# Seven products for eight in one half of the gate and up projections of a float32 decoder trunk

## Chip, core and metric

One NeuronCore of a Trainium2 chip runs the whole program in one launch. The metric is the device time of one execution in microseconds (us), weights and inputs read from HBM. The engines are called PE (TensorE), DVE (VectorE), ACT (ScalarE), POOL (GpSimd) and SP (SyncE, which issues nearly all DMAs) in the profile's rows.

## What is computed

256 tokens of width 1024 go through two layers. Each layer has a half-step SwiGLU feed-forward step, a mixing step with two kinds of attention, a second feed-forward step of the same form, and a gated input embedding. All is float32.

```python
def swiglu(x, w_gate, w_up, w_down):
    return (jax.nn.silu(x @ w_gate) * (x @ w_up)) @ w_down

def hybrid_layer(h, p_i, ...):          # D_MODEL = 1024, D_FF = 2816, DEPTH = 2
    h = h + 0.5 * swiglu(rms_norm(h, ffn1_norm), ffn1_w_gate, ffn1_w_up, ffn1_w_down)
    ...                                  # mixing: projections, two attentions, w_out
    h = h + 0.5 * swiglu(rms_norm(h, ffn2_norm), ffn2_w_gate, ffn2_w_up, ffn2_w_down)
    gate = jax.nn.sigmoid(rms_norm(h, ple_norm) @ w_ple_gate)
    h = h + gate * (p_i @ w_ple_proj)
    return h
```

## The kernel before

**Matmuls.** A float32 operand is split in two: a high part rounded to fp32r (`wh`, by ACT) and the rest (`wl`, by DVE). `mm3` (L213 to L220) issues three matmuls of 512 columns for one product: high by high (L217), low by high and high by low (L218, L219; `x` split alike into `h` and `l`). The tokens (128 at a time, one half `t` of the 256) are stationary, the weights are the moving operand.

**Weights.** All weights lie in HBM in units of 128 x 2048, in the order of use. `Unit.load` (L120) brings a piece of 128 x 1024 into one of 7 raw buffers (L128, queue of SP), and splits it into one of 8 pairs `wh`, `wl` (L132 on ACT, L133 on DVE). So ACT and DVE can be up to eight pieces ahead of PE, and the DMAs up to seven pieces ahead of them. A raw buffer is free again when DVE has split it; a pair is free again when PE has used it.

**A feed-forward step** (`ffn`, L482). The four steps are called a0, b0 (layer 0) and a1, b1 (layer 1). The 2816 columns of gate and up are worked in five blocks of 512 and a last one of 256. A block runs over K = 1024 in 8 chunks of 128 and over two halves of the tokens: 16 `mm3` into the banks `g` of PSUM and 16 into the banks `u`, 96 matmuls. `gated` (L485) applies silu on ACT and multiplies on DVE (`pr`, L491); `Gates.add` (L453) has PE transpose the result (four transposes `ft` for each half of tokens) and splits it into `fh`, `fl` for the down projection. `soon` puts such late work behind a number of matmuls.

**Sevens.** Three blocks (1 to 3) of the down projection already go as seven products for eight: with a 2 x 2 partition of weights and of gates, `Seven.operands` (L177) makes the weights' seven operands from four raw pieces with four sums on DVE (L168, in the raw buffers) and seven splits (L173, L174), `Gates.sums` (L409) makes the sums of the gates, and the products add up in seven banks of PSUM over the three blocks. Each product of a block is two `mm3`, six matmuls.

**Order.** Each engine and queue runs its own list in order. The lists are set when the program is built: a scheduler places the instructions engine by engine, so that a matmul of later work can stand ahead of one that would wait. PSUM has 8 banks, taken in turn.

## Time and profile before

| | |
|---|---|
| three runs | 1017.68, 1017.71, 1018.44 us (median 1017.71) |
| the profiled execution | 1019.1 us, of it 1017.3 us span from the first to the last instruction |
| TensorE's granted clock | 0.997 on the mean, 1.00 in the feed-forward steps |
| PE busy | 1004.5 us (99%) in 5106 matmuls and transposes |
| DVE busy | 753.1 us (74%) |
| ACT busy | 618.8 us (61%) |
| DMA | 187.41 MB, mean 184 GB/s |

The profile is of one execution; its times are us from the start of the span. An engine's row gives the start of an instruction and how long it took until its result was there. The engines take up the next instruction before that, so what an instruction costs an engine that never waits is the distance between the starts of two neighbours, and busy times of PE are no measure of what its matmuls cost.

### The profile page before, as it was taken

What the parts mean: (1) busy time and instruction counts of PE and PEld (TensorE: products, weight loads), DVE (VectorE), ACT (ScalarE), POOL (GpSimd) and SP (SyncE); (2) the same over time, 40 slices, a digit from 0 to 9 for tenths busy, and PEclk for the clock granted to TensorE, in tenths of its full rate; (3) what the DMA queues carried; (4) which work ended last, traced back from release to release, by engine and by line L of the source; (5) the groups of instructions that cost most, each with busy time, mean ns of one, the idle gap of its engine ahead of it and who ended that gap; (6) DMA issues with size and microseconds to landing.
All of it is one profiled execution on the core that took longest, in us unless ns stands there. A gap on an engine that the chain in (4) does not pass through costs nothing.

```text
span 1017.3 us, 13800 instructions
## 1 busy us (share of the span) xinstructions
PE 1004.5 (99%) x5106; PEld 849.9 (84%) x5106; DVE 753.1 (74%) x1051; ACT 618.8 (61%) x950; POOL 8.4 (1%) x13
## 2 busy tenths in 40 slices
PE   9999999999999999999999999999999999999996
PEld 7888888899888888888888888888998888888885
DVE  5776789976766666799865667899676756678994
ACT  5855566767575555557764555656766745556663
POOL 0000000000100000000000000000010000000000
PEclk9999999999999999999999999999999999999998
DMA  9875346674246555456765554557623465544641
GB/s 316 319 269 187 125 151 225 221 249 149 84 145 209 184 187 175 135 177 228 235 208 181 182 177 135 186 192 264 228 84 125 153 219 184 186 149 138 214 154 43
DMA packets 53492, 187.41 MB, mean 184 GB/s; under 512 B 6064, under 2 KB 6192, under 8 KB 53424
## 3 DMA queue, kind: packets, MB, share of 16 engines
q1 hardware_dynamic: 52992, 185.95, 54.2%
q8 instruction: 40, 0.66, 0.3%
q10 hardware_dynamic: 432, 0.57, 0.2%
q14 instruction: 28, 0.23, 0.1%
HBM read 185.45 MB, written 1.05 MB: 183 GB/s over the span
## 4 chain that ended last, share of the span: by engine, by line
PE 96%; DMA 2%; ACT 1%; DVE 0%; issue 0%; SPq 0%; ACTq 0%
PE g_a L217 4%; PE g_a L219 4%; PE g_b L219 4%; PE g_b L217 4%; PE g_b L218 4%; PE g_a L218 4%; PE u_a L217 4%; PE u_b L217 4%; PE u_a L218 4%; PE u_b L218 4%; PE u_b L219 4%; PE u_a L219 4%; PE d_b L219 3%; PE d_b L218 3%; PE d_b L217 3%; PE d_a L219 2%
## 5 line engine op out<-in xcount | busy, mean ns | idle before, releaser
L133 DVE TENSOR_TENSOR wl<-raw,wh 128x1024 fp32r<-128x1024 f32 (+1 forms) x306 | 362.3, 1197 | 161.0 <-ACT wh L132 159.5
L132 ACT ACTIVATE wh<-raw 128x1024 fp32r<-128x1024 f32 (+1 forms) x306 | 313.5, 1036 | 187.1 <-PE u_b L219 43.8
L173 ACT ACTIVATE wh<-raw 128x1024 fp32r<-128x1024 f32 x84 | 88.5, 1061 | 77.3 <-DVE raw L168 35.9
L174 DVE TENSOR_TENSOR wl<-raw,wh 128x1024 fp32r<-128x1024 f32 x84 | 100.4, 1221 | 11.7 <-ACT wh L173 11.0
L168 DVE TENSOR_TENSOR raw<-raw,raw 128x1024 f32<-128x1024 f32 x48 | 58.6, 1221 | 14.4 <-DMA raw<-in_w 12.1
L217 PE MATMUL d_a<-wh,fh_a 128*128 128x512 f32 x108 | 42.7, 396 | 0.0
L217 PE MATMUL d_b<-wh,fh_b 128*128 128x512 f32 x108 | 42.7, 396 | 0.0
L219 PE MATMUL d_b<-wh,fl_b 128*128 128x512 f32 x108 | 42.1, 390 | 0.0
L219 PE MATMUL d_a<-wh,fl_a 128*128 128x512 f32 x108 | 42.1, 390 | 0.0
L218 PE MATMUL d_a<-wl,fh_a 128*128 128x512 f32 x108 | 42.1, 389 | 0.0
L218 PE MATMUL d_b<-wl,fh_b 128*128 128x512 f32 x108 | 42.1, 389 | 0.0
L217 PE MATMUL g_a<-wh,x0h 128*128 128x512 f32 x96 | 38.0, 398 | 1.1 <-ACT x0h L262 1.1
L217 PE MATMUL g_b<-wh,x_mix0h 128*128 128x512 f32 x96 | 38.4, 400 | 0.0
L217 PE MATMUL g_b<-wh,x_mix1h 128*128 128x512 f32 x96 | 38.4, 400 | 0.0
L217 PE MATMUL g_a<-wh,xe0h 128*128 128x512 f32 x96 | 38.4, 400 | 0.0
L219 PE MATMUL g_a<-wh,xe0l 128*128 128x512 f32 x96 | 37.6, 391 | 0.0
L219 PE MATMUL g_b<-wh,x_mix1l 128*128 128x512 f32 x96 | 37.5, 390 | 0.0
L219 PE MATMUL g_b<-wh,x_mix0l 128*128 128x512 f32 x96 | 37.5, 390 | 0.0
L218 PE MATMUL g_b<-wl,x_mix0h 128*128 128x512 f32 x96 | 37.4, 390 | 0.0
L218 PE MATMUL g_b<-wl,x_mix1h 128*128 128x512 f32 x96 | 37.4, 390 | 0.0
L218 PE MATMUL g_a<-wl,xe0h 128*128 128x512 f32 x96 | 37.4, 390 | 0.0
L219 PE MATMUL g_a<-wh,x0l 128*128 128x512 f32 x96 | 37.3, 390 | 0.0
(454 smaller groups left out, 2551.2 us busy)
## 6 DMA issues: line engine op xcount, KB each, us to landing
raw<-in_w SPq DMA_DIRECT2D x338, 512.0 KB, 4.2
raw<-in_w SPq DMA_DIRECT2D x16, 256.0 KB, 5.2
xin<-in_xT SPq DMA_DIRECT2D x4, 256.0 KB, 5.3
h<-in_xr SPq DMA_DIRECT2D x2, 512.0 KB, 9.2
p<-in_pT SPq DMA_DIRECT2D x2, 256.0 KB, 4.9
fg<-in_fgain SPq DMA_DIRECT2D x1, 512.0 KB, 4.8
out_h<-hg SPq DMA_DIRECT2D x2, 256.0 KB, 2.3
out_h<-hg ACTq DMA_DIRECT2D x2, 256.0 KB, 2.7
```

What stands on the lines that cost most here:

```text
L132: nc.scalar.activation(wh[:, a], r[:, a], AF.Copy),
L133: nc.vector.tensor_tensor(wl[:, a], r[:, a], wh[:, a].bitcast(F32), ALU.subtract),
L168: nc.vector.tensor_tensor(self.raw[o], self.raw[a], self.raw[b], op)
L173: newest_wh[0] = nc.scalar.activation(wh, r, AF.Copy)
L174: nc.vector.tensor_tensor(wl, r, wh.bitcast(F32), ALU.subtract)
L217: nc.tensor.matmul(o, ah, bh, start=start, stop=False, **kw)
L218: nc.tensor.matmul(o, ah, bl, start=False, stop=False, **kw)
L219: newest_mm[0] = nc.tensor.matmul(o, al, bh, start=False, stop=stop, **kw)
```

## The change

In step a0 block 3, and in each of the other three steps blocks 1 and 3, the first half of K (chunks 0 to 3) is worked as seven products for eight. The partition is 2 x 2: the weights by K (256 and 256 rows) and by gate and up (512 and 512 columns), x by K and by token half. Seven products of two `mm3` take the place of eight.

`operands_own_first` loads the four pieces and yields the operands in the order 1, 7, 6, 5, 2, 4, 3. Products 1, 7, 6, 5 start banks of their own. Product 2 is added to bank `p1`, product 4 to `p7`, product 3 to `p5`, once the bank's first content has been read: ACT copies `p1` to `u`; DVE adds `p6` to it, makes `v` = `u` + `p7`, and `e` = `p5` - `v` (`u` and `v` are the halves of the tile printed as `ch`, `e` is in `cl`). The second half of K (chunks 4 to 7) goes on as before, 48 matmuls, and adds on to the same banks: gate on to `p1` and `p7`, up on to `p5` and a new bank `c22`. Three more sums on DVE then give the gate's second half and the two halves of up.

`x_sums` runs once in each step: one sum of the two parts of x over chunks 0 to 3, four sums of 128 x 256 on DVE, two splits on each of ACT and DVE. The weights' units are packed in the order of the new pieces; their number stays.

```diff
--- before.py
+++ after.py
@@ -30,6 +30,13 @@
 
 
 SEVEN = (1, 2, 3)
+
+
+def wide_sevens(first):
+
+    return (3,) if first else (1, 3)
+
+
 
 F_TAGS = ("sbq", "sbk", "v", "vm", "n0h", "n0l", "n1h", "n1l", "f4h", "f4l", "f5h", "f5l")
 
@@ -190,6 +197,25 @@
             self.sum(b21, b11, b21)
             yield 4, self.parts(b21)
 
+        def operands_own_first(self):
+
+            b11, b12, b21, b22 = range(4)
+            self.load(b11)
+            yield 1, self.parts(b11)
+            self.load(b12)
+            self.load(b22)
+            self.sum(b12, b12, b22)
+            yield 7, self.parts(b12)
+            self.sum(b11, b11, b12)
+            yield 6, self.parts(b11)
+            self.sum(b12, b11, b22, ALU.subtract)
+            yield 5, self.parts(b12)
+            self.load(b21)
+            yield 2, self.parts(b21)
+            self.sum(b11, b11, b21)
+            yield 4, self.parts(b11)
+            yield 3, self.parts(b22)
+
 
     due = []
     pe = [0.0]
@@ -493,8 +519,73 @@
 
             return silu, rest
 
+        xs = []
+
+        def x_sums():
+
+            v = f_p.tile([P, 4, T], F32, tag="f5h", name=f"xf_{tag}")
+            xh, xl = (q[:, 0:4].bitcast(F32) for q in x)
+            nc.vector.tensor_tensor(v, xh, xl, ALU.add)
+            a11, a12, a21, a22 = (v[:, k : k + 2, t * P : (t + 1) * P] for t in range(2) for k in (0, 2))
+            two = [wt(f"w{2 + k}", f"xsum{k}_{tag}") for k in range(2)]
+            s1, s2, s3, s4 = (two[k // 2][:, k % 2].rearrange("p (a b) -> p a b", a=2) for k in range(4))
+            nc.vector.tensor_tensor(s1, a21, a22, ALU.subtract)
+            nc.vector.tensor_tensor(s2, s1, a11, ALU.subtract)
+            nc.vector.tensor_tensor(s3, a11, a21, ALU.subtract)
+            nc.vector.tensor_tensor(s4, s2, a12, ALU.add)
+            xs.extend(f_p.tile([P, 4, T], F32R, tag=f"f4{q}", name=f"xs{q}_{tag}") for q in "hl")
+            for k in range(2):
+                sh, sl = (q[:, 2 * k : 2 * k + 2] for q in xs)
+                nc.scalar.activation(sh, two[k], AF.Copy)
+                nc.vector.tensor_tensor(sl, two[k], sh.bitcast(F32), ALU.subtract)
+
+        def x_of(p, j):
+            if p in (1, 2, 4):
+                return tok(x, j + 2 * (p != 1), int(p == 4))
+            return both(xs, slice(None), {5: 0, 6: 1, 7: 2, 3: 3}[p], slice(j * P, (j + 1) * P))
+
+        def wide_seven(i):
+
+            if not xs:
+                x_sums()
+            p = {k: bank(f"p{k}_{tag}{i}") for k in (1, 7, 6, 5)}
+            e2 = tuple(f_p.tile([P, 4, T], F32, tag=f"f5{q}", name=f"c{q}_{tag}{i}").rearrange("p a b -> p (a b)") for q in "hl")
+            u, v, e = e2[0][:, :512], e2[0][:, 512:], e2[1][:, :512]
+            own = (1, 7, 6, 5)
+            to = {**p, 2: p[1], 4: p[7], 3: p[5]}
+            for q, (wh, wl) in Seven().operands_own_first():
+                for j in range(2):
+                    c = slice(j * 512, (j + 1) * 512)
+                    mm3(to[q], x_of(q, j), (wh[:, c], wl[:, c]), q in own and j == 0, q in own and j == 1, skip_group_check=True)
+                if q == 1:
+                    nc.scalar.copy(u, p[1])
+                elif q == 6:
+                    nc.vector.tensor_tensor(u, u, p[6], ALU.add)
+                    nc.vector.tensor_tensor(v, u, p[7], ALU.add)
+                elif q == 5:
+                    nc.vector.tensor_tensor(e, p[5], v, ALU.subtract)
+            c22 = bank(f"c22_{tag}{i}")
+
+            def half_mm(u, banks):
+                for k in range(4):
+                    for t in range(2):
+                        mm3(banks[t], tok(x, 4 + k, t), u.at(k, 0, 512), banks[t] is c22 and k == 0, k == 3, skip_group_check=True)
+
+            ug, uu = Unit(4), Unit(4)
+            half_mm(ug, (p[1], p[7]))
+            nc.vector.tensor_tensor(v, u, p[7], ALU.add)
+            rests = [gated(i, 0, p[1], u)[1], gated(i, 1, v, e)[1]]
+            half_mm(uu, (p[5], c22))
+            nc.vector.tensor_tensor(u, p[5], u, ALU.subtract)
+            nc.vector.tensor_tensor(e, e, c22, ALU.add)
+            for r in rests:
+                r(1.4)
+
         for i in range(NBLK):
             last = i == NBLK - 1
+            if i in wide_sevens(feed is not None):
+                wide_seven(i)
+                continue
             g = [bank(f"g_{tag}_{i}{t}") for t in range(2)]
             sub = {"sub": 2} if feed and i == 0 else {}
             wg = wide([Unit(4, **sub) for _ in range(2)])
@@ -1005,6 +1096,10 @@
             wg, wu, wd = (i[f"{n}_w_{s}"][L] for s in ("gate", "up", "down"))
             for j in range(NBLK - 1):
                 m = ar(512 * j, 512 * j + 512)
+                if j in wide_sevens(L == 0 and n == "ffn1"):
+                    units.extend(np.concatenate([cols(v[k : k + 256], m) for v in (wg, wu)], axis=1) for k in (0, 256))
+                    units.extend(cols(v[512:], m) for v in (wg, wu))
+                    continue
                 wide(wg, m)
                 wide(wu, m)
             m = ar(DFF - 256, DFF)
```

Three places in the engines' lists, in the program before and in the changed one. The lines of the changed kernel are other numbers for the same code (L133 is now L140, L174 is L181, L168 is L175, L217 to L219 are L243 to L245, L491 is L517, L468 is L494, L262 is L288).

DVE in step b0, from the gating of block 0 (`pr`) on, before:

```order
L491 SCALAR_TENSOR_TENSOR pr_b0_00_3047<-u_b0_00_2871,hr_mix0_2754,s_b0_00_2971 128x512
L491 SCALAR_TENSOR_TENSOR pr_b0_01_3051<-u_b0_01_2872,hr_mix0_2754,s_b0_01_2973 128x512
L133 TENSOR_TENSOR wl54_1_0_129_3202<-raw54_1_0_129_3203,wh54_1_0_129_3201 128x1024
L468 TENSOR_TENSOR fl_b0_0_3050<-ft_b0_00_3069,fh_b0_0_3049 128x4x128
L133 TENSOR_TENSOR wl55_0_0_130_3230<-raw55_0_0_130_3231,wh55_0_0_130_3229 128x1024
L468 TENSOR_TENSOR fl_b0_0_3050<-ft_b0_01_3082,fh_b0_0_3049 128x4x128
L133 TENSOR_TENSOR wl55_1_0_131_3275<-raw55_1_0_131_3276,wh55_1_0_131_3274 128x1024
```

and now:

```order
L517 SCALAR_TENSOR_TENSOR pr_b0_00_3081<-u_b0_00_2905,hr_mix0_2788,s_b0_00_3005 128x512
L517 SCALAR_TENSOR_TENSOR pr_b0_01_3085<-u_b0_01_2906,hr_mix0_2788,s_b0_01_3007 128x512
L181 TENSOR_TENSOR wl7_51_0_130_3188<-raw7_51_0_3107,wh7_51_0_130_3187 128x1024
L181 TENSOR_TENSOR wl7_51_3_131_3198<-raw7_51_3_3129,wh7_51_3_131_3197 128x1024
L494 TENSOR_TENSOR fl_b0_0_3084<-ft_b0_00_3119,fh_b0_0_3083 128x4x128
L140 TENSOR_TENSOR wl53_0_0_132_3209<-raw53_0_0_132_3210,wh53_0_0_132_3208 128x1024
L494 TENSOR_TENSOR fl_b0_0_3084<-ft_b0_01_3142,fh_b0_0_3083 128x4x128
L563 TENSOR_TENSOR ch_b01_3105<-ch_b01_3105,p6_b01_3103 128x512
L140 TENSOR_TENSOR wl53_1_0_133_3227<-raw53_1_0_133_3228,wh53_1_0_133_3226 128x1024
L564 TENSOR_TENSOR ch_b01_3105<-ch_b01_3105,p7_b01_3102 128x512
L140 TENSOR_TENSOR wl54_0_0_134_3250<-raw54_0_0_134_3251,wh54_0_0_134_3249 128x1024
L566 TENSOR_TENSOR cl_b01_3106<-p5_b01_3104,ch_b01_3105 128x512
```

Behind the gating the list held splits and the two results `fl` of block 0; now the splits of the operands of products 4 and 3 stand there (`wl7_51_0_130`, `wl7_51_3_131`), and the three sums from the shared banks between the splits of the second half of K.

PE in step b0 at the start of block 1, before:

```order
L217 MATMUL g_b0_10_3053<-wh51_0_0_122_3057,x_mix0h_2751 128x512
L218 MATMUL g_b0_10_3053<-wl51_0_0_122_3058,x_mix0h_2751 128x512
L219 MATMUL g_b0_10_3053<-wh51_0_0_122_3057,x_mix0l_2752 128x512
L217 MATMUL g_b0_11_3054<-wh51_0_0_122_3057,x_mix0h_2751 128x512
L218 MATMUL g_b0_11_3054<-wl51_0_0_122_3058,x_mix0h_2751 128x512
```

and now, behind products 1, 7, 6, 5 and 2 of that block (the first three rows are the second half of K, added to `p1`; then comes product 4, into `p7`):

```order
L245 MATMUL p1_b01_3101<-wh53_0_0_132_3208,x_mix0l_2786 128x512
L243 MATMUL p1_b01_3101<-wh53_0_0_132_3208,x_mix0h_2785 128x512
L244 MATMUL p1_b01_3101<-wl53_0_0_132_3209,x_mix0h_2785 128x512
L243 MATMUL p7_b01_3102<-wh7_51_0_130_3187,x_mix0h_2785 128x512
L244 MATMUL p7_b01_3102<-wl7_51_0_130_3188,x_mix0h_2785 128x512
L245 MATMUL p7_b01_3102<-wh7_51_0_130_3187,x_mix0l_2786 128x512
```

Five matmuls of the second half of K (the last three of them are shown) stand ahead of product 4, and two ahead of product 3 in the same way; all 4667 rows of PE's list now stand against 4709 before.

ACT at the start of step a1, from the table load on, before (`xt01` is the turned h of chunks 4 to 7, token half 0; the last `xe0h` of it is chunk 7):

```order
L100 ACT_TABLE_LOAD
L262 ACTIVATE xe0h_4400<-xt01_e0_4656,g_sb_80 128x128
L274 ACTIVATE y_ple00_4688<-hr_ple0_4403 128x1
L132 ACTIVATE wh88_1_0_206_4849<-raw88_1_0_206_4851 128x1024
L262 ACTIVATE xe0h_4400<-xt01_e0_4656,g_sb_80 128x128
L298 ACTIVATE junk_ple0_11_4683,hss_ple0_4402<-h_82 128x512
L275 ACTIVATE y_ple00_4688<-y_ple00_4688 128x1
```

and now:

```order
L107 ACT_TABLE_LOAD
L288 ACTIVATE xe0h_4488<-xt01_e0_4744,g_sb_80 128x128
L139 ACTIVATE wh88_1_0_215_4937<-raw88_1_0_215_4939 128x1024
L288 ACTIVATE xe0h_4488<-xt01_e0_4744,g_sb_80 128x128
L324 ACTIVATE junk_ple0_11_4771,hss_ple0_4490<-h_82 128x512
L300 ACTIVATE y_ple00_4776<-hr_ple0_4491 128x1
L288 ACTIVATE xe0h_4488<-xt11_e0_4827,g_sb_80 128x128
L301 ACTIVATE y_ple00_4776<-y_ple00_4776 128x1
L539 ACTIVATE xsh_a1_4969<-xsum0_a1_4963 128x512
L288 ACTIVATE xe0h_4488<-xt01_e0_4744,g_sb_80 128x128
```

Chunks 5 to 7 stand behind the table load now, where before only 6 and 7 did, and the squares of h (`junk`), a first part of the other token half (`xt11`) and a split of the sums of x (`xsh`) stand ahead of chunk 7.

## Rows read from the trace of the kernel before

**Rows 1.** The page of the profile: the span, part 1 (busy time, share of the span and instructions of each engine), TensorE's granted clock by slice in part 2 (tenths of full speed), part 4 (the chain that ended last, by engine) and the weight loads of part 6 (count, KB, median us from issue to landing).

```profile
span 1017.3 us, 13800 instructions
PE 1004.5 (99%) x5106; PEld 849.9 (84%) x5106; DVE 753.1 (74%) x1051; ACT 618.8 (61%) x950; POOL 8.4 (1%) x13
...
PEclk9999999999999999999999999999999999999998
...
PE 96%; DMA 2%; ACT 1%; DVE 0%; issue 0%; SPq 0%; ACTq 0%
...
raw<-in_w SPq DMA_DIRECT2D x338, 512.0 KB, 4.2
```

**Rows 2.** Timeline of TensorE in blocks 2 and 3 of step a0: start us, us, engine, line, operation, out<-in, shape, count. The first three rows are the first and last of the u matmuls of block 2 and the first g matmul of block 3, 48 matmuls after the first; the other two are four transposes and the second matmul behind them.

```profile
85.33 0.39 PE L217 MATMUL u_a<-wh,x0h 128*128 128x512 f32 x1
...
95.99 0.39 PE L219 MATMUL u_a<-wh,x0l 128*128 128x512 f32 x1
96.21 0.39 PE L217 MATMUL g_a<-wh,x0h 128*128 128x512 f32 x1
...
97.58 0.60 PE L462 MATMUL ft_a<-c_sb,pr_a 128*128 128x128 f32 x4
98.24 0.39 PE L218 MATMUL g_a<-wl,x0h 128*128 128x512 f32 x1
```

**Rows 3.** Busy time by stretch: the stretch, its length, then for PE, PEld, DVE, ACT and POOL busy us (count), TensorE's granted clock as a share of full speed, mean DMA share, GB/s. The first stretch is the down projection of step a0 where it works in sevens, the other two are blocks 1 and 2 of step b0.

```profile
137.00:173.00 36.00, 36.00 (x161) 29.81 (x160) 33.23 (x30) 23.24 (x24) 0.00 (x0) 1.00 0.58 190
317.83:340.50 22.67, 22.67 (x105) 18.80 (x104) 12.34 (x13) 10.84 (x12) 0.00 (x0) 1.00 0.55 186
340.50:363.20 22.70, 22.70 (x105) 18.80 (x104) 14.78 (x19) 12.03 (x15) 0.00 (x0) 1.00 0.55 184
```

**Rows 4.** Groups of instructions by line and form: line, engine, operation, out<-in, shapes, count | busy us, mean ns of one | idle us of the engine just before them, and what ended it.

```profile
L133 DVE TENSOR_TENSOR wl<-raw,wh 128x1024 fp32r<-128x1024 f32 x290 | 352.1, 1225 | 153.7 <-ACT wh L132 152.3
L132 ACT ACTIVATE wh<-raw 128x1024 fp32r<-128x1024 f32 x290 | 304.0, 1059 | 182.1 <-PE u_b L219 43.8 <-PE u_a L219 34.7 <-issue 22.5
...
L168 DVE TENSOR_TENSOR raw<-raw,raw 128x1024 f32<-128x1024 f32 x48 | 58.6, 1221 | 14.4 <-DMA raw<-in_w 12.1 <-issue 1.8
...
L468 DVE TENSOR_TENSOR fl_b<-ft_b,fh_b 128x512 fp32r<-128x512 f32 x14 | 9.6, 689 | 0.7
```

**Rows 5.** Timeline of VectorE in step a0 (columns as in Rows 2). Rows that follow each other without idle time give the distance from one start to the next, which is what an instruction holds the engine for.

```profile
59.89 1.29 DVE L434 TENSOR_TENSOR sxl_a<-sum_a,sxh_a 128x512 fp32r<-128x512 f32 x2
...
80.50 0.42 DVE L427 TENSOR_TENSOR sum_a<-sum_a,ft_a 128x256 f32<-128x256 f32 x1
80.83 0.42 DVE L428 TENSOR_TENSOR sum_a<-ft_a,sum_a 128x256 f32<-128x256 f32 x1
...
141.41 4.63 DVE L174 TENSOR_TENSOR wl<-raw,wh 128x1024 fp32r<-128x1024 f32 x4
145.95 2.48 DVE L168 TENSOR_TENSOR raw<-raw,raw 128x1024 f32<-128x1024 f32 x2
...
175.77 0.69 DVE L582 TENSOR_TENSOR v_a<-u_a,p_a 128x512 f32<-128x512 f32 x1
176.38 0.68 DVE L580 TENSOR_TENSOR a_a<-p_a,u_a 128x512 f32<-128x512 f32 x1
```

**Rows 6.** Timeline of VectorE at the start of step b0: the last parts of x, the last weight split of block 0, and the two gatings of block 0.

```profile
303.90 0.61 DVE L263 SCALAR_TENSOR_TENSOR x_mix0l<-xt_mix,g_sb,x_mix0h 128x128 fp32r<-128x128 f32 x2 [1.91 <-ACT x_mix0h L262]
...
316.40 1.23 DVE L133 TENSOR_TENSOR wl<-raw,wh 128x1024 fp32r<-128x1024 f32 x1 [1.49 <-ACT wh L132]
317.54 1.40 DVE L491 SCALAR_TENSOR_TENSOR pr_b<-u_b,hr_mix,s_b 128x512 f32<-128x512 f32 x2
```

**Rows 7.** Timeline of TensorE at the same place: the first matmul of block 1 of step b0, and the transposes of block 0's result behind its first six matmuls.

```profile
317.83 0.39 PE L217 MATMUL g_b<-wh,x_mix0h 128*128 128x512 f32 x1
...
319.19 0.60 PE L462 MATMUL ft_b<-c_sb,pr_b 128*128 128x128 f32 x4
```

**Rows 8.** Who waited for whom in the whole span: engine, instruction <- what it waited for: us in total, times, longest us.

```profile
DVE wl L133 <- ACT wh L132: 159.5, 127, 5.8
...
ACT wh L132 <- PE u_b L219: 43.8, 28, 1.7
...
DVE raw L168 <- DMA raw<-in_w: 12.1, 8, 2.0
```

**Rows 9.** Timeline of ScalarE at the start of step a1: the table load before the last parts of x, and the last part of token half 0 (chunk 7).

```profile
508.15 1.28 ACT L100 ACT_TABLE_LOAD   x1
...
510.75 0.35 ACT L262 ACTIVATE xe0h<-xt_e,g_sb 128x128 fp32r<-128x128 f32 x1
```

**Rows 10.** Timeline of TensorE at the same place: the first matmuls of chunks 6 and 7 of x for token half 0.

```profile
511.73 0.39 PE L217 MATMUL g_a<-wh,xe0h 128*128 128x512 f32 x1
512.42 0.39 PE L217 MATMUL g_a<-wh,xe0h 128*128 128x512 f32 x1
```

**Rows 11.** Timeline of VectorE near the start of the program, in block 0 of step a0.

```profile
10.84 2.50 DVE L133 TENSOR_TENSOR wl<-raw,wh 128x512 fp32r<-128x512 f32 x4
...
16.86 0.69 DVE L133 TENSOR_TENSOR wl<-raw,wh 128x512 fp32r<-128x512 f32 x1 [0.83 <-ACT wh L132]
```

**Rows 12.** Timeline of TensorE at the same place: the second matmul of chunk 2 of x for u, which reads the weights' low part.

```profile
13.42 0.39 PE L218 MATMUL u_a<-wl,x0h 128*128 128x512 f32 x1
```

## The prediction

> **What bounds the kernel now.** I read the page first: PE is busy for 99% of the span, the chain that ended last is 96% PE, and the granted clock is full in every slice but the last [rows 1]. So time is won where PE has fewer matmuls, if the others keep up. What a matmul costs is read from starts. Block 2 of step a0 has 48 of them from 85.33 to 96.21 us [rows 2]: 10.88/48 = **0.2267 us** each, although each row lists 0.39, which is its latency. Four transposes put in between cost 98.24 - 97.58 - 0.2267 = 0.43 us. Next the busy times by stretch: in a block of 22.7 us DVE works 12.3 to 14.8 us and ACT 10.8 to 12.0 [rows 3]. The waits say that DVE waits for ACT and ACT for PE to give back a pair of weight buffers [rows 8]: both stand eight pieces ahead and idle there. Where the down projection works in sevens DVE is busy 33.23 of 36.00 us, and PE still has no gap [rows 3]: that lead carries a stretch in which DVE is nearly the bound.
>
> **What goes.** Seven products of two `mm3` for eight: 2 x 3 = 6 matmuls less in a block of 96. One block in a0, two in each of the others: 7 blocks, 42 matmuls, which is also the difference of the two lists of PE (4709 and 4667 rows). 42 x 0.2267 = **9.52 us**. The stationary and moving shapes and the transposes are the same. The Trainium skill, "TensorE: Matmul & The Clock Gate", section "Back-to-back issue gap", gives about 131 ns for a 512 column matmul in a sustained stream and 216 ns for one alone; by these the 42 would be 5.5 or 9.1 us. The trace has 226.7 in a sustained stream of these split operands, so the page's lower figure does not hold here.
>
> **What comes, on DVE and ACT.** What an instruction holds DVE for, from starts [rows 5]: a 1024 split (145.95 - 141.41)/4 = 1.135, a 1024 sum the same, or 1.22 behind the sum it reads [rows 4, 5], 512 columns 0.61 to 0.66, 256 columns 0.33. A block gets 11 splits for 8, 4 sums of weights and 6 sums from the banks: 3 x 1.135 + 4 x 1.135 + 6 x 0.64 = 11.8 us more. The sums of x cost 1.14 + 4 x 0.33 + 2 x 0.62 = 3.7 us once in a step. ACT gets three splits (1.06 [rows 4]), a copy of 0.6, and two of 0.57 for x: under 5 us in a block, with 10 idle. So DVE has 14.8 + 11.8 = 26.6 us of work in a block in which PE now needs 22.7 - 1.36 = 21.3. It is 5.3 us short, 9.0 with the sums of x, and what covers it is the lead: a product takes PE only 6 x 0.2267 = 1.36 us, a piece of the old kind 12 x 0.2267 = 2.72, and eight pairs are held ready. The block between has 22.7 - 14.8 = 7.9 us to spare and refills them.
>
> **The tightest place walked through: block 1 of step b0.** DVE has the last part of x that the sums need at 303.90 + 2 x 0.26 = 304.42 [rows 6]. Then its list holds the sum of x 1.14, one part of x 0.26, four small sums 1.32, two splits of sums 1.24, five weight splits 5.68 and three weight sums 3.5: 13.1 us, to 317.6. That is when the last u of block 0 ends and the gating starts in both programs (317.54 [rows 6]). Gating 1.40, splits of products 4 and 3 2.27, `fl` 0.62, a split behind ACT 1.3, `fl` 0.62: 323.85. `p6` is added by 324.5, another split to 325.6, `v` by **326.25**. PE starts block 1 at 317.83 [rows 7]; five products are 6.80, the transposes of block 0 0.9: 325.53, then five matmuls put ahead of the wait, 1.13: it asks for `p7` at **326.66**. The margin is 0.4 us. Product 3 asks for `p5` at 326.66 + 1.36 + 0.45 = 328.5, and `e` is there at 326.25 + 1.14 + 0.65 = 328.0: again 0.4. If such a margin is lost, what waits behind product 4 is all of PE. In the same way block 3 comes out over a microsecond early (no sums of x, a whole block of lead); a0's block 3, which has the sums of x, 0.2 us late; b1 is b0 again. For these waits I take 0.2 for a0 and 0.1 for each of the other five places with little margin, **0.7 us**; the bounds are 0 and, if every wait came 1 us later than walked, about 0.6 to 1.0 in each of seven blocks, 4 to 7.
>
> **The moved work at the start of a1.** Before, ACT gives chunk 7 of x at 510.75 behind the table load at 508.15 [rows 9], and PE takes chunks 6 and 7 from 511.73 and 512.42 [rows 10]. Now a 1.14 us sum of x goes ahead of the gate's sum in h on DVE, chunk 5 goes behind the table load, and `junk`, `xt11` and `xsh` ahead of chunk 7. By the same durations the load ends at 509.8, chunk 5 at 510.1, a split at 511.1, chunk 6 at 511.4, its low part on DVE at 512.6; `junk` 512.0, `xsh` 513.0, chunk 7 513.3. PE waits some 0.4 us at chunk 6 and 0.5 at chunk 7: **0.9 us**, bounds 0 and 1.5.
>
> **What is hidden.** At the start of a0 the sum of x goes between two splits: the second low part of chunk 2 ends at 10.84 + 0.69 + 1.14 + 0.7 = 13.4, and PE reads it at 13.42 [rows 11, 12]; DVE's next pause, 0.83 us at 16.86 [rows 11], takes most of it up. No cover beyond that; if it fails, 0.2 us. SP issues as many loads as before (338 of 512 KB, 4.2 us to landing [rows 1]). A raw buffer of a seven stays taken longer, up to product 4's split, and loads behind it in SP's queue wait with it; the piece that then comes into the buffer is the fourth of the second half of K, needed 18 us later. Sums on DVE wait for a landing in 8 places already, 12.1 us in all, without a gap on PE [rows 8]. POOL has no part in it.
>
> **Sum.** 9.52 - 0.7 - 0.9 = 7.9 us. The profiled execution, 1019.1 us with 1017.3 of span, would be 1011.2 with 1009.4. It lies 1.4 above the median of the runs, 1017.71, so the median becomes **1009.8**.
>
> **Rivals.**
> - *No added wait anywhere*: 1017.71 - 9.52 = 1008.2. For it: PE's lack of gaps in the down projection's sevens. Against: margins of 0.4 and the place in a1.
> - *The shared banks make PE wait in every block.* Products 4 and 3 need banks that DVE reads last, and DVE is late by a microsecond through handoffs from ACT: 4 to 7 us back, 1012.2 to 1015.2. The Trainium skill, "Perfetto Trace Analysis", section "Matmuls", speaks for this and against the change: independent groups should rotate through the banks, so that one is emptied while the next is filled. The down projection's sevens, which also turn to a bank again within a block but read it only at the end, cannot show it. Against: the matmuls put ahead of both products.
> - *Slower: the lead does not hold and DVE sets the pace.* Uncovered, the shortage is 7 x 5.3 + 4 x 3.7 = 52 us. The change loses from the point where more than 9.52/52 = 18% of it comes through; at a quarter it is 1008.2 + 13 = 1021. It decides at the first seven of b0 and b1, where x is late. Against: 33.23 of 36 us busy without a gap [rows 3].
> - *PE's listed time is what counts*: 42 x 0.39 = 16.4 us, 1001.3. The starts speak against it.
>
> **Chances.** Forecast (1008.6 to 1011.5) 0.58, no wait 0.20, shared banks 0.15, DVE as bound 0.05, listed time 0.02. A measurement of this kernel tells 0.2%, 2.0 us, from no change. Faster: all but the DVE case and the worst of the shared banks, 0.91; the same 0.05; slower 0.04. The range leaves out the DVE case, the listed time and the upper part of the shared banks: **1007.8 to 1013.2**.
>
> **What would show it.** PE's starts still 0.227 us apart and 42 rows fewer; a block of a step that changes shorter by 1.36 us (22.7 to about 21.3); a gap of some 0.9 us on PE some 5 us into a1's first block, and hardly any at products 4 and 3; DVE's busy time up by 7 x 11.8 + 4 x 3.7, about 95 us by starts. It is wrong if PE's gaps in front of `p7` and `p5` add up to over 3 us, or if ACT and DVE no longer wait for PE's buffers in the blocks between.

## Result: 7 us faster, and the profile after

| | before | after |
|---|---|---|
| median of the runs (lowest to highest) | 1017.75 us (1017.68 to 1018.44) | **1010.80 us** (1010.20 to 1011.79) |
| ratio, 95% interval | | 0.9931 [0.9914, 0.9948] |
| the profiled execution, span | 1019.1, 1017.3 us | 1010.7, 1008.9 us |

Predicted were 1009.8 us, from 1007.8 to 1013.2. The page of the changed kernel, for [rows 1]: span, busy times, granted clock, chain, weight loads.

```profile
span 1008.9 us, 13852 instructions
PE 996.9 (99%) x5064; PEld 842.3 (83%) x5064; DVE 839.9 (83%) x1170; ACT 645.7 (64%) x986; POOL 7.4 (1%) x13
...
PEclk9999999999999999999999999999999999999998
...
PE 96%; ACT 1%; DVE 1%; DMA 1%; issue 1%; POOL 0%; DVEq 0%; ACTq 0%; POOLq 0%
...
raw<-in_w SPq DMA_DIRECT2D x338, 512.0 KB, 4.6
```

PE has 42 rows less and is still the chain; DVE has 119 instructions and 86.8 us of busy time more. The groups of the weight splits and sums, for [rows 4], and the waits, for [rows 8]; the first of the waits is one of the kernel before, of its down projection's sevens:

```profile
L140 DVE TENSOR_TENSOR wl<-raw,wh 128x1024 fp32r<-128x1024 f32 (+1 forms) x278 | 324.5, 1191 | 59.3 <-ACT wh L139 58.8
...
L181 DVE TENSOR_TENSOR wl<-raw,wh 128x1024 fp32r<-128x1024 f32 x133 | 159.3, 1220 | 24.4 <-ACT wh L180 23.6
...
L175 DVE TENSOR_TENSOR raw<-raw,raw 128x1024 f32<-128x1024 f32 x76 | 92.7, 1219 | 14.9 <-DMA raw<-in_w 13.2 <-issue 1.2
```

```profile
DVE wl L174 <- ACT wh L173: 11.0, 12, 1.3
```

```profile
DVE wl L140 <- ACT wh L139: 58.8, 53, 5.4
...
DVE raw L175 <- DMA raw<-in_w: 13.2, 9, 2.9
...
PE ft_a L488 <- DVE pr_a L517: 1.5, 1, 1.5
```

DVE's idle time behind ACT's splits has fallen from 159.5 [rows 8] and 11.0 us to 58.8 and 23.6, by 88.1 us in all: that is what paid for the new work. The last row is new: PE waits for DVE's gating, once.

Busy time in blocks 1, 2 and 3 of b0, for [rows 3], each block from its first matmul to the first of the next.

```profile
316.12:337.45 21.33, 21.33 (x100) 17.68 (x98) 19.96 (x22) 15.85 (x18) 0.00 (x0) 1.00 0.82 276
337.45:360.14 22.69, 22.69 (x105) 18.80 (x104) 19.87 (x25) 11.89 (x15) 0.00 (x0) 1.00 0.45 164
360.14:381.48 21.34, 21.34 (x99) 17.57 (x98) 20.06 (x26) 15.36 (x19) 0.00 (x0) 1.00 0.64 213
```

DVE is busy 20.0 of 21.3 us in each of the two sevens and 19.9 of 22.7 in the block between them, where blocks 1 and 2 had 12.3 and 14.8. The block between carries 5.1 us more than before: splits and sums of the next seven.

The time by step, from the start of a step's first matmul to that of the next (a0 from the start of the span; mix is the mixing step), in every profiled execution of this study. PE's list in the mixing steps is the same in all of them.

| kernel | a0 | mix0 | b0 | a1 | mix1 | b1 |
|---|---|---|---|---|---|---|
| before | 187.91 | 107.23 | 182.46 | 182.11 | 107.65 | 182.46 |
| e5, before again | 187.45 | 106.92 | 182.46 | 182.10 | 106.64 | 182.46 |
| **after** | 186.78 | 106.65 | 179.80 | 181.39 | 106.84 | 179.82 |
| e1, after again | 186.66 | 106.66 | 179.80 | 181.69 | 106.73 | 179.80 |
| e2, sum moved in a1 | 187.00 | 106.70 | 179.82 | 179.79 | 107.09 | 179.82 |
| e3, two moved | 186.85 | 106.65 | 179.80 | 179.75 | 107.06 | 179.80 |
| e4, block 3 alone | 187.91 | 106.65 | 181.18 | 181.18 | 107.32 | 181.19 |
| e6, three blocks | 186.31 | 106.66 | 185.78 | 184.93 | 107.10 | 186.32 |
| e7, splits doubled | 187.48 | 106.96 | 183.18 | 180.72 | 107.05 | 183.94 |
| e8, sums of x alone | 187.91 | 106.65 | 182.46 | 182.41 | 106.66 | 182.46 |
| e9, banks turned at once | 189.14 | 106.95 | 189.59 | 189.18 | 106.66 | 189.57 |
| e10, three moved | 186.31 | 106.64 | 179.80 | 179.63 | 106.65 | 179.80 |

b0 and b1 lose 2.66 us each, two blocks of 1.33: twelve matmuls are 2.72. a1 loses only 0.4 to 0.7 with the same twelve matmuls less. The place is at the start of its block 2. Timelines of the changed kernel there: PE, then DVE, then SP's queue.

```profile
549.35 0.39 PE L245 MATMUL g_a<-wh,xe0l 128*128 128x512 f32 x1
551.21 0.63 PE L488 MATMUL ft_a<-c_sb,pr_a 128*128 128x128 f32 x4 [1.47 <-DVE pr_a L517]
```

```profile
542.71 1.23 DVE L140 TENSOR_TENSOR wl<-raw,wh 128x1024 fp32r<-128x1024 f32 x1 [0.40 <-ACT wh L139]
546.84 1.22 DVE L175 TENSOR_TENSOR raw<-raw,raw 128x1024 f32<-128x1024 f32 x1 [2.91 <-DMA raw<-in_w]
547.99 1.22 DVE L140 TENSOR_TENSOR wl<-raw,wh 128x1024 fp32r<-128x1024 f32 x1
549.12 0.68 DVE L579 TENSOR_TENSOR ch_a<-p_a,ch_a 128x512 f32<-128x512 f32 x1
549.72 0.68 DVE L580 TENSOR_TENSOR cl_a<-cl_a,c_a 128x512 f32<-128x512 f32 x1
550.32 0.74 DVE L517 SCALAR_TENSOR_TENSOR pr_a<-ch_a,hr_ple,s_a 128x512 f32<-128x512 f32 x1
```

```profile
537.64 3.93 SPq L172 DMA_DIRECT2D raw<-in_w  x4
```

The first weight sum of block 3's seven (L175) stands in DVE's list ahead of block 1's last sums from the banks (L579, L580) and of its gating (`pr`). Its last piece comes from the four loads issued between 537.64 and 541.57 and lands just ahead of the sum's start at 546.84; DVE stands for 2.91 us, everything behind the sum is late, and PE gets the transposes 1.63 us late (1.86 less the usual 0.23). In b0 and b1 the scheduler had put that sum behind the gating.

### The profile page after: what moved, and what is told of

Read it like the earlier page. It is cut to its first block, busy times and chain, and to the rows that moved or that the text cites. A ratio compares the mean times of both kernels' runs of the same rounds, so it can differ in the third digit from the quotient of the medians.

```text
span 1008.9 us, 13852 instructions
## 1 busy us (share of the span) xinstructions
PE 996.9 (99%) x5064; PEld 842.3 (83%) x5064; DVE 839.9 (83%) x1170; ACT 645.7 (64%) x986; POOL 7.4 (1%) x13
## 4 chain that ended last, share of the span: by engine, by line
PE 96%; ACT 1%; DVE 1%; DMA 1%; issue 1%; POOL 0%; DVEq 0%; ACTq 0%; POOLq 0%
PE p_b L243 3%; PE p_b L245 3%; PE p_b L244 3%; PE g_a L243 3%; PE g_a L245 3%; PE g_a L244 3%; PE g_b L245 3%; PE g_b L243 3%; PE g_b L244 3%; PE d_b L245 3%; PE d_b L244 3%; PE d_b L243 3%; PE u_a L244 3%; PE u_a L245 3%; PE u_a L243 3%; PE d_a L244 3%
## 5 line engine op out<-in xcount | busy, mean ns | idle before, releaser
L140 DVE TENSOR_TENSOR wl<-raw,wh 128x1024 fp32r<-128x1024 f32 (+1 forms) x278 | 324.5, 1191 | 59.3 <-ACT wh L139 58.8
L139 ACT ACTIVATE wh<-raw 128x1024 fp32r<-128x1024 f32 (+1 forms) x278 | 282.8, 1035 | 120.3 <-DMA raw<-in_w 14.4
L180 ACT ACTIVATE wh<-raw 128x1024 fp32r<-128x1024 f32 x133 | 139.6, 1060 | 123.2 <-DVE raw L175 58.7
L181 DVE TENSOR_TENSOR wl<-raw,wh 128x1024 fp32r<-128x1024 f32 x133 | 159.3, 1220 | 24.4 <-ACT wh L180 23.6
L175 DVE TENSOR_TENSOR raw<-raw,raw 128x1024 f32<-128x1024 f32 x76 | 92.7, 1219 | 14.9 <-DMA raw<-in_w 13.2
L243 PE MATMUL d_a<-wh,fh_a 128*128 128x512 f32 x108 | 42.7, 396 | 0.0
L243 PE MATMUL d_b<-wh,fh_b 128*128 128x512 f32 x108 | 42.7, 396 | 0.0
L245 PE MATMUL d_b<-wh,fl_b 128*128 128x512 f32 x108 | 42.1, 390 | 0.0
L245 PE MATMUL d_a<-wh,fl_a 128*128 128x512 f32 x108 | 42.1, 390 | 0.0
L243 PE MATMUL g_a<-wh,x0h 128*128 128x512 f32 x80 | 31.9, 401 | 0.0
L245 PE MATMUL g_a<-wh,x0l 128*128 128x512 f32 x80 | 31.0, 390 | 0.0
L244 PE MATMUL g_a<-wl,x0h 128*128 128x512 f32 x80 | 31.0, 390 | 0.0
L243 PE MATMUL g_b<-wh,x_mix0h 128*128 128x512 f32 x64 | 25.6, 400 | 0.0
L243 PE MATMUL g_b<-wh,x_mix1h 128*128 128x512 f32 x64 | 25.6, 400 | 0.0
L243 PE MATMUL g_a<-wh,xe0h 128*128 128x512 f32 x64 | 25.5, 401 | 0.0
L245 PE MATMUL g_a<-wh,xe0l 128*128 128x512 f32 x64 | 25.1, 392 | 0.0
L244 PE MATMUL u_a<-wl,x0h 128*128 128x512 f32 x64 | 25.0, 391 | 0.0
L245 PE MATMUL g_b<-wh,x_mix0l 128*128 128x512 f32 x64 | 25.0, 390 | 0.0
L245 PE MATMUL g_b<-wh,x_mix1l 128*128 128x512 f32 x64 | 25.0, 390 | 0.0
```

Of the source, the lines that this page charges most:

```text
L139: nc.scalar.activation(wh[:, a], r[:, a], AF.Copy),
L140: nc.vector.tensor_tensor(wl[:, a], r[:, a], wh[:, a].bitcast(F32), ALU.subtract),
L175: nc.vector.tensor_tensor(self.raw[o], self.raw[a], self.raw[b], op)
L180: newest_wh[0] = nc.scalar.activation(wh, r, AF.Copy)
L181: nc.vector.tensor_tensor(wl, r, wh.bitcast(F32), ALU.subtract)
L243: nc.tensor.matmul(o, ah, bh, start=start, stop=False, **kw)
```

## Experiments

The theory (A): PE sets the time, a seven gives 1.36 us, and what is missing stands at single places, most of it at the sum just shown. Rivals: the waits are chance; DVE as a whole is the bound; the shared banks cost; a slow landing is itself what PE waits for.

**e1, the changed kernel again** (no edit).

> The changed kernel as it is, once more, so that the next kernels can be compared with it on one chip. Theory A (PE sets the time; what the change loses lies in three places): about 7 to 8.4 us faster than before; on PE again one wait of about 1.6 us beyond the usual distance in step a1, ahead of the transposes of block 1's result (1.86 us from start to start at 549 us), and 0.27 us near 13 us in step a0; from product to product of a seven no distance over 0.35. Rival B (these waits are chance of one execution, a slow landing): the 1.6 us wait is gone or stands elsewhere. Of the starts of the two mixing steps, where before had 1.01 us and 0.54 + 0.71 us between neighbours and after 0.26 and 0.43, either theory leaves open whether the gain of about 1.4 us comes again.

1010.71 us, ratio 0.9935 [0.9922, 0.9949]. The distance from start to start on PE in a1 is there again, 2.14 us at 549.25; near 13 us again 0.38 and 0.34. So the wait in a1 is not chance of one execution.

**e2, the sum behind the gating in a1.** An order between two instructions of DVE; PE's list stays the same. Up to the gating only the sum moves; behind it a few rows of DVE and ACT change places. (In the edits, `...` stands for lines left out.)

```diff
-            self.sum(b12, b12, b22)
+            first = self.sum(b12, b12, b22)
+            if behind is not None:                 # a1 and b0, b1: pr of block 1, when i == 3
+                after(first, behind)
...
```

> Only the order of DVE's list changes, and only in the second feed-forward pair of blocks of a1: the first weight sum of block 3's seven comes behind the gating products of block 1, where it stood in front of them. Theory A (that sum waits 2.91 us for a landing, and the sums from the banks and the gating products stand behind it, so PE's transposes come 1.6 us late): the distance of 1.86 us on PE in a1 falls to 0.35 or less, and the kernel is 1.6 us faster than the changed one, 8.5 to 10 us faster than before. Rival C (DVE is the bound over the whole pair of blocks, and the wait only shows where its list is late): the wait comes back on PE within the next block, at product 7 or at the next transposes, and the time stays within 0.3 us of the changed kernel. Rival D (the landing itself is what PE waits for): the sum, and with it product 7 of block 3, still comes too late, and 1 us or more stands at block 3 instead.

1010.12 us, 0.9923 [0.9911, 0.9936]. a1 falls from 181.69 to 179.79, by 1.9 us, and no distance over 0.38 is left in it. DVE and PE of this kernel at that place:

```profile
545.80 1.22 DVE L140 TENSOR_TENSOR wl<-raw,wh 128x1024 fp32r<-128x1024 f32 x1 [1.54 <-ACT wh L139]
546.95 0.68 DVE L582 TENSOR_TENSOR ch_a<-p_a,ch_a 128x512 f32<-128x512 f32 x1
547.55 0.68 DVE L583 TENSOR_TENSOR cl_a<-cl_a,c_a 128x512 f32<-128x512 f32 x1
548.14 0.74 DVE L520 SCALAR_TENSOR_TENSOR pr_a<-ch_a,hr_ple,s_a 128x512 f32<-128x512 f32 x1
...
550.60 1.22 DVE L175 TENSOR_TENSOR raw<-raw,raw 128x1024 f32<-128x1024 f32 x1
```

```profile
549.67 0.39 PE L247 MATMUL g_a<-wh,xe0l 128*128 128x512 f32 x1
549.90 0.60 PE L490 MATMUL ft_a<-c_sb,pr_a 128*128 128x128 f32 x4
```

The sum now waits for nothing, `pr` starts 2.2 us earlier, and PE goes on at 0.23. The wait did not come back later in the step, so DVE as the bound over the pair of blocks is out, and so is the landing as such. The total moved less than expected, 0.6 us by the medians and 1.1 by the spans: mix1 took 0.36 us more and a0 0.34 more than in e1, with the same PE lists. The mechanism is shown by the step; that it is worth all of 1.9 us in the median is not.

**e3, also a0's sum of x later.**

```diff
-            nc.vector.tensor_tensor(v, xh, xl, ALU.add)
+            s0 = nc.vector.tensor_tensor(v, xh, xl, ALU.add)
+            if feed is not None:
+                after(s0, mark[0])                 # last weight split of block 0
...
```

> As the one before, and in step a0 the sum of x over chunks 0 to 3 comes behind the last weight split of block 0 instead of between its splits for chunk 2. Theory A: PE's two distances of 0.39 and 0.34 us at 13 us become the usual 0.23, so 0.27 us more is won: 1.9 us faster than the changed kernel, 9 to 10 us faster than before, and nothing appears in block 3 of a0, which needs the sums 60 us later. Rival: DVE has no pause in block 0 either way, and the 0.27 us stands a few us later, at the first splits of block 1.

1009.62 us, 0.9919 [0.9906, 0.9933]. The two distances near 13 us are gone, but a0 is no shorter (186.85 against 186.66): this execution had 0.60 and 0.42 at 6 us, when PE waited for the first landings. The start of the program varies by more than the 0.27 us in question; what this order is worth stays open.

**e4, block 3 alone.**

```diff
-    return (3,) if first else (1, 3)
+    return (3,)
```

> Block 3 alone is worked in sevens, in each of the four steps (4 blocks in place of 7; the weights are packed to match). Theory A: PE has 24 matmuls less than before, 24 x 0.2267 = 5.4 us; less 0.27 us in a0 and at most 0.3 us in a1: 4.8 us by itself, and up to 1.4 us more if the mixing steps start as in the changed kernel: 4.8 to 6.2 us faster than before. With block 1 of a1 of the old kind no sum waits ahead of its gating, and the 1.86 us distance is not there. If DVE's work were what limits the sevens (rival C), each of the four blocks would give more than a seventh of what the changed kernel gave, over 1.2 us each with no wait anywhere, and the changed kernel's missing part would be spread over its blocks 1.

1013.79 us, 0.9963 [0.9951, 0.9975], 3.9 us faster than before, 0.9 less than the lower end of what was expected. b0 and b1 give 1.28 and 1.27 for their one block, a1 0.93. a0's list is that of the changed kernel, but it took 187.91: at 39 us, ahead of any seven, PE waited 1.0 us for a split whose piece had landed late, in this execution alone. One seven gives what half of two gives: no interplay of the blocks, with a block of the old kind between.

**e5, the kernel before again** (no edit).

> The kernel before, once more, for the starts of the two mixing steps. From the first v matmul to the first kn matmul the profiled execution of before took 70.36 us (layer 0) and 70.78 us (layer 1); the changed kernel and three variants took 69.80 to 69.85 and 69.88 to 70.47, although the lists of PE there are the same. Theory B1 (a landing that is late by chance in one execution): another execution of before has 69.8 to 70.4 in layer 0, so this part of the gain is not the change's. Theory B2 (the change moves the time at which the loads are issued, so the wait goes): 70.36 and 70.78 come again within 0.1 us.

1017.27 us, one run. mix0 106.92 and mix1 106.64 where the first execution had 107.23 and 107.65: the changed kernel's are 106.65 to 106.84. So the 1.4 us that the profile of after gains at the mixing steps are mostly chance of the profiled execution of before: B1 holds for mix1, and for half of mix0. A late landing is shown for one place, a row of ACT in mix0 of that execution; in e5 and in the changed kernel the same instruction has no wait:

```profile
194.75 1.06 ACT L132 ACTIVATE wh<-raw 128x1024 fp32r<-128x1024 f32 x1 [0.63 <-DMA raw<-in_w]
```

**e6, sevens in blocks 1, 2 and 3.**

```diff
-    return (3,) if first else (1, 3)
+    return (3,) if first else (1, 2, 3)
```

> Blocks 1, 2 and 3 as sevens in b0, a1 and b1, block 3 in a0 (10 blocks in place of 7, the weights packed to match): no block of the old kind stands between. Theory A (PE sets the time as long as the lead lasts): a seven gives 1.33 us net, so b0 and b1 fall from 179.8 to 178.5 us and the time to about 1006.7, provided that the lead carries three sevens in a row. Rival C (DVE): three sevens and the sums of x are 3 x 26.6 + 3.7 = 83.5 us of DVE's work beside 3 x 21.3 = 64 us of PE's, 19.5 us short. Eight pairs of buffers are worth 8 x 1.36 = 10.9 us of sevens; 9 to 16 us more is not covered, and each of the three steps becomes 5 to 10 us longer instead: b0 at 185 to 190 us, the time 1022 to 1040, with waits on PE for wl and for the shared banks in blocks 2 and 3.

1026.5 us, 1.0083 [1.0068, 1.0098]: slower than before. b0 is 185.78, 7.3 us over the 178.5 of an unbroken lead. PE at block 3 of b0:

```profile
365.47 0.50 PE L243 MATMUL p_b<-wh,x_mix0h 128*128 128x512 f32 x1 [0.45 <-ACT wh L180]
366.88 0.47 PE L243 MATMUL p_b<-wh,x_mix0h 128*128 128x512 f32 x1 [0.92 <-ACT sum_b L451]
368.54 0.49 PE L244 MATMUL p_b<-wl,xsh_b 128*128 128x512 f32 x1 [1.18 <-DVE wl L181]
```

Here DVE and ACT set the pace. Of the 19.5 us that DVE was reckoned short, some 12 were covered in b0, where the granted clock stayed at 1.00. The change needs the block of the old kind between two sevens.

**e7, four splits of each seven done twice.**

```diff
-            nc.vector.tensor_tensor(wl, r, wh.bitcast(F32), ALU.subtract)
+            for _ in range(2 if more else 1):      # more: operands 7, 6, 5, 4
+                nc.vector.tensor_tensor(wl, r, wh.bitcast(F32), ALU.subtract)
...
```

> The low parts of four of a seven's operands (7, 6, 5 and 4) are computed twice over, with the same result: 4 x 1.135 = 4.5 us more of DVE's work in each of the seven blocks, nothing else. In the changed kernel's trace v of b0's block 1 is done 0.65 us before product 4 asks for its bank, and e 0.73 us before product 3; in three other blocks there is a start distance of 0.28 us, no margin at all. Theory A (the margins at the shared banks are what the change lives on): four of seven blocks and more lose 3.5 to 4.5 us each, b0 goes from 179.8 to 185 us or more, the time to 1020 to 1040. Rival (DVE, busy 83% of the span, has slack and the lead takes it up): under 1 us in a step, the time 1011 to 1013.

1018.77 us, 1.0005 [0.9996, 1.0014]; neither range held. The scheduler also answered the added work with other lists, PE's included. In a1 it put block 3's first weight sum behind the gating by itself, so a1 is compared with e2: 0.9 us longer. a0 is 0.8 longer, b0 and b1 are 3.4 and 4.1. PE in block 1 of b0, and DVE and ACT there:

```profile
324.86 0.47 PE L244 MATMUL p_b<-wh,x_mix0h 128*128 128x512 f32 x1
326.44 0.50 PE L244 MATMUL p_b<-wh,x_mix0h 128*128 128x512 f32 x1 [1.10 <-ACT wh L139]
...
327.64 0.50 PE L245 MATMUL p_b<-wl,x_mix0h 128*128 128x512 f32 x1 [0.47 <-DVE wl L182]
```

```profile
324.03 0.69 DVE L565 TENSOR_TENSOR ch_b<-ch_b,p_b 128x512 f32<-128x512 f32 x1
```

```profile
323.43 2.01 ACT L180 ACTIVATE wh<-raw 128x1024 fp32r<-128x1024 f32 x2 [1.89 <-DVE raw L175]
```

From start to start, 2.2 us are lost here, 0.4 at the next transposes and 0.7 in block 3. The 2.2 us are not waits for a shared bank: `v` was there at 324.72, ahead of product 4's first matmul at 324.86. PE waited for a high part of the second half of K, late because ACT had stood 1.89 us for a weight sum of DVE, and for the low part of product 4. So the place that the prediction had walked, the first seven behind a late x, breaks first and most, but at the weight splits: of 4.5 us more work about half comes through there in b0 and b1, and 0 to 1.2 us in the other five blocks. DVE has less room than the rival had it and more than the theory. Some 1.5 us of b1's 4.1 are the granted clock (last section).

**e8, the sums of x alone** (blocks of the old kind throughout; the sums are computed and not used).

```diff
-    return (3,) if first else (1, 3)
+    return ()
...
-            if i in wide_sevens(feed is not None):
-                wide_seven(i)
-                continue
+            if i in ((3,) if feed is not None else (1, 3)) and not xs:
+                x_sums()
```

> The kernel before with the sums of x added (one sum, four small sums, two splits on each of ACT and DVE, once in each step) and no block in sevens: the sums are computed and not used. Theory A: b0 and b1 stay at 182.46 us within 0.1; a0 is 0.27 us longer (distances of 0.39 and 0.34 us near 13 us on PE), a1 0.3 to 0.4 us longer (chunks 6 and 7 of x, which ACT gives later), all in all 0.6 to 0.7 us slower than before, not counting chance at the starts of the mixing steps. Prediction's term for the same: 0.9 us in a1 and up to 0.2 in a0. Rival: nothing, since the distances in the changed kernel come from the sevens' own splits.

1017.82 us, 0.9997 [0.9988, 1.0007]. b0 and b1 to the hundredth as before, a1 0.30 longer. In a0 no distance near 13 us, although DVE's list has the sum at the same place: PE had started later here (0.60 and 0.43 at 6 us), and the 0.27 did not show. So the sums cost 0.3 us in a1, and in a0 what the start leaves them.

**e9, product 4 directly behind product 6.**

```diff
             yield 6, self.parts(b11)
             self.sum(b12, b11, b22, ALU.subtract)
-            yield 5, self.parts(b12)
             self.load(b21)
-            yield 2, self.parts(b21)
             self.sum(b11, b11, b21)
             yield 4, self.parts(b11)
+            yield 5, self.parts(b12)
+            yield 2, self.parts(b21)
...
+                if q != 1:
+                    chain[0] = newest_mm[0]        # the next product's first matmul stays behind it
...
```

> Product 4, which goes into the bank of product 7, directly behind product 6, then 5, 2 and 3, and the products kept in that order on PE with no matmul of the second half of K put between; before, 5, 2 and five matmuls of the second half stood between 6 and 4. Same work, 7 blocks. Rival S of the prediction (the turn of a shared bank costs PE a wait): product 4 asks for its bank 4.1 us of products and 0.9 us of transposes after the start of block 1 in b0, about 321.1, while DVE's list gives v at 324.3 to 325.4: 3 to 4.5 us of wait in block 1 of b0 and b1, 1.5 us (two sums of 0.6 us behind product 6) up to 4 in the others, b0 at 184 to 187 us instead of 179.8, the time at 1022 to 1036. If the turn itself were cheap (DVE's sums done by the time), under 1 us in a block and 1011 to 1017.

1040.0 us, 1.0223 [1.0209, 1.0237], above the range. PE in block 1 of b0, then stretches of the same place (stretch, length, busy us and count of PE, PEld, DVE, ACT, POOL, granted clock, DMA share, GB/s):

```profile
323.56 0.40 PE L248 MATMUL p_b<-wh,xsl_b 128*128 128x512 f32 x1
327.20 0.47 PE L243 MATMUL p_b<-wh,x_mix0h 128*128 128x512 f32 x1 [3.25 <-DVE ch_b L569]
```

```profile
323.79:327.20 3.41, 0.17 (x1) 0.03 (x1) 3.41 (x6) 1.91 (x3) 0.00 (x0) 1.00 0.81 270
327.20:328.46 1.26, 1.25 (x5) 1.02 (x6) 1.26 (x2) 0.00 (x0) 0.00 (x0) 0.98 0.71 263
328.46:331.80 3.34, 3.34 (x9) 2.65 (x8) 3.25 (x4) 1.17 (x2) 0.00 (x0) 0.50 0.81 291
331.80:336.00 4.20, 4.20 (x20) 3.41 (x19) 3.08 (x4) 3.08 (x3) 0.00 (x0) 1.00 0.84 283
```

Turned at once, a bank costs PE 2.8 to 3.4 us in each of the seven blocks. That is the bank's turn behind DVE's list and not the two sums alone: DVE was busy for all of the 3.41 us above, mostly with splits and `fl` that stand ahead of the sums and between them. The expectation had that. What it lacked is behind it: in six of the seven places the granted clock then fell to 0.50, and some eight matmuls came at 0.427 us, 1.5 to 1.7 us more.

**e10, three orders moved**: e3, and in a1 ACT's splits of the sums of x behind the last part of x.

```diff
-                nc.scalar.activation(sh, two[k], AF.Copy)
+                q = nc.scalar.activation(sh, two[k], AF.Copy)
+                if tag == "a1":
+                    after(q, newest_split[0])
...
```

> The two moves of before (the weight sum of a1's block 3 behind the gating of block 1, the sum of x of a0 behind block 0's weight splits), and in a1 the first split of the sums of x on ACT behind the last part of x instead of ahead of chunk 7. Theory A: a1, 179.75 to 179.79 us with the sum moved, loses another 0.2 to 0.3 us (its three distances of 0.33 to 0.36 us near 508 us go back to 0.23), 179.5; the time 1009.3 to 1009.6, 8 to 8.6 us faster than before. Rival: the distances come from the earlier table load and from chunk 5 behind it, which stay, and a1 stays at 179.75.

**1008.95 us**, 0.9915 [0.9901, 0.9928], the fastest of all, 1.8 us by the median below the changed kernel. a1 is 179.63, 0.12 us less than in e3, where 0.2 to 0.3 was expected: the last of the three distances is gone, 0.38 and 0.34 stay. So the split accounts for a third of what a1's start loses. The rest was not taken apart; the earlier table load and chunk 5 behind it, the rival of the expectation, are still there.

## Why the prediction was right, and where it was not

**The matmuls: right.** 42 rows less, starts 0.227 us apart, 1.33 of 1.36 us in a block of b0 and b1. The rival by PE's listed time (16.4 us) is out.

**The walk of b0's block 1: right, to 0.2 us.** The changed kernel's DVE and PE there:

```profile
323.65 0.68 DVE L564 TENSOR_TENSOR ch_b<-ch_b,p_b 128x512 f32<-128x512 f32 x1
...
325.39 0.68 DVE L566 TENSOR_TENSOR cl_b<-p_b,ch_b 128x512 f32<-128x512 f32 x1
```

```profile
324.98 0.39 PE L243 MATMUL p_b<-wh,x_mix0h 128*128 128x512 f32 x1
...
326.80 0.39 PE L243 MATMUL p_b<-wh,xsh_b 128*128 128x512 f32 x1
```

b0 begins 1.71 us earlier than before. With that taken off, `v` was due at 324.54 and was there at 324.33; `p7` was due to be asked for at 324.95 and was at 324.98. The margins are 0.65 and 0.73 where 0.4 was walked. But this was not the tightest place. Block 3, which the prediction had "over a microsecond early" in all steps but a0, had no margin: DVE, then PE, in block 3 of b0.

```profile
367.31 0.68 DVE L564 TENSOR_TENSOR ch_b<-ch_b,p_b 128x512 f32<-128x512 f32 x1
```

```profile
367.88 0.66 PE L243 MATMUL p_b<-wh,x_mix0h 128*128 128x512 f32 x2
368.38 0.40 PE L244 MATMUL p_b<-wl,x_mix0h 128*128 128x512 f32 x1
```

`v` is there at 367.99, and product 4 starts with the second of the two matmuls, at 368.10; in block 3 of all four steps the two lie 0.10 to 0.13 us apart. DVE's list there also holds sums of block 2's gates, which the prediction does not name. It cost next to nothing, since PE then started at once, but the walk had looked at the wrong block.

**The waits at the shared banks, 0.7 us: too large.** Three starts at such places, all in blocks 3, are 0.28 to 0.29 us from their neighbour, 0.17 us in all. The rival of the shared banks did not come true in the change: between the two uses of a bank PE has other work. The Trainium skill, "Perfetto Trace Analysis", section "Matmuls", says that independent groups of matmuls should rotate through different banks, so that one is emptied while the next is filled. e9 agrees with it where the work between is taken away: 2.8 to 3.4 us a block.

**The start of a1, 0.9 us: too large.** Three distances of 0.36, 0.34 and 0.33 are 0.34 us together; e8 has 0.30 for the sums alone.

```profile
507.69 0.40 PE L244 MATMUL g_a<-wl,xe0h 128*128 128x512 f32 x1
508.05 0.50 PE L245 MATMUL g_a<-wh,xe0l 128*128 128x512 f32 x1
508.38 0.73 PE L243 MATMUL g_a<-wh,xe0h 128*128 128x512 f32 x2
```

**What was called hidden: the step that failed.** "Sums on DVE wait for a landing in 8 places already, 12.1 us in all, without a gap on PE" was true of before and carried over to the new sums without looking at what stands behind each of them. The waits are hardly more (13.2 us in 9 places), but one of them now has the gating behind it: 1.6 and 1.9 us in two executions, the largest single loss, and gone with the order (e2). The raw buffers were checked for who needs the next piece, not DVE's list for who is behind the sum. The sum of x in a0, put at 0.2 us if the cover fails, cost 0.27 and 0.26 in the two executions of the changed kernel, and nothing in e6, whose a0 has the same lists.

**DVE as the bound: rightly small for this change, and near.** Its busy time went up by 86.8 us, where about 95 by starts were forecast (the forecast's own terms add up to 97.4; the page counts listed times, so the two are not the same measure). In block 2 of b0 ACT still waits 8.4 us for PE's buffers and DVE 2.8 us for ACT, so the sign named for this rival did not come. The lead covers two sevens with a block between; with three in a row it does not, and the kernel is slower than before (e6).

**The sum.** 9.52 - 0.17 - 0.34 - 0.27 - 1.6 to 1.9 = 6.8 to 7.1 us; the medians differ by 6.95 and 6.98 (e1). That the forecast of 7.9 lay only 1 us off owes something to errors that cancel: two waits sized 1.1 us too large, one of 1.6 to 1.9 us not seen. The profiled spans differ by 8.4 us, which flatters the change: 1.4 us of it are at the mixing steps, and e5 has most of that without the change.

## To carry to other kernels

When work is added to an engine's list, ask of each instruction that waits for a DMA not only whether its own result is in time, but what stands behind it in that list and who waits for that; the cure can be an order of two instructions. Work that is more than an engine can do within one block can still be free if a lead is there and a block between refills it: add up the shortage over the blocks in a row and hold it against the lead. And compare two profiles step by step, with a second execution of each: here steps with the same lists differed by up to 1 us and more from one execution to the next.

## Not expected of the hardware

- In e9 a single wait of PE of 3.2 to 3.6 us from start to start was followed, at once or after up to 1.5 us of matmuls at the normal distance, by some 3.3 us at a granted clock of 0.50 (1.2 GHz), with 0.427 us from start to start (six of seven places; in a0, behind 3.0 us, the clock stayed at 1.00). So there the wait cost about half as much again behind itself. After the single waits of 1.86 and 2.14 us in the changed kernel's a1 it stayed at 1.00.
- The length of the waits alone does not decide it. In e7 the same two waits, 1.57 and 0.87 us from start to start, left the clock at 1.00 in block 1 of b0 and were followed by 0.50 in block 1 of b1 (the two rows below). In e6 it fell behind waits of 0.9 to 1.7 us in a1 (for over 5 us) and in b1, and stayed at 1.00 behind a longer row of such waits in b0. What decides between these is open.
- Executions of the same lists differ, at least in part by late landings: a0 took 186.31 to 187.91 us in five executions whose a0 has the same lists (after, e1, e2, e4, e6), mix1 106.64 and 107.65 us in two executions of before.

```profile
328.00:332.00 4.00, 4.00 (x19) 3.30 (x18) 4.00 (x4) 3.24 (x4) 0.00 (x0) 1.00 0.69 238
828.80:831.40 2.60, 2.60 (x7) 1.98 (x6) 2.60 (x3) 2.01 (x3) 0.00 (x0) 0.50 0.64 216
```
